# Down by a scheme of seven products, row sums on GpSimd, sample P.V in block-diagonal form

## The chip, the cores and the metric

The kernel runs on one core of one Trainium2 chip. The metric is the device time of one execution in microseconds; the median of three runs before the change is 2301.47 (2296.75 to 2304.92).

## What is computed

Two layers of a streaming encoder over 1024 prompt frames and 8 x 16 sample frames, all in float32. Each layer mixes (windowed attention beside a pooling path) and then runs a gated convolutional feed-forward. The parts that the change touches, cut from the reference:

```python
def conv_ffn(x, prev, w_up, conv_w, conv_b, w_down):
    h = x @ w_up
    ...
    gate, val = jnp.split(c, 2, axis=-1)
    y = (jax.nn.silu(gate) * val) @ w_down
    return y, full[:, -(CONV_W - 1):]
...
        keys = jnp.concatenate([cache_k, k], axis=1)
        vals = jnp.concatenate([cache_v, v], axis=1)
        attn = sink_attention(q, keys, vals, sinks, None)
...
    x = x + f
```

D_MODEL is 1024, D_FF is 2816 (22 tiles of 128). `state_conv` holds the last two up-projected rows of each of the 8 sample streams.

## The kernel before

Rows are cut into nine tiles `t` of 128: 0 to 7 are the prompt, 8 is the 128 sample rows. Every large product is made in float32 precision from operands split into a rounded part `hi` and a rest `lo`: `mm3` issues three matmuls, L152 (hi.hi), L153 (hi.lo) and L154 (lo.hi). ScalarE makes `hi` by a cast, VectorE `lo` by a subtraction.

A layer has three stages. The **mixer** runs from the input projection to the output projection; its pieces (projection columns `k`, `u`, `o`, pooling `p`, norms `n` and `m`, attention steps `L`, side loads `cw`, `sc`) have keys in `PLAN`, and `arrange` sorts them by key under their preconditions. **Up** runs over 22 tile pairs `i` of `w_up`; each takes seven products (a scheme of seven instead of eight, `PRODUCTS`) in two halves of four `mm3`, 168 matmuls 288 columns wide. VectorE adds the products up (L921), convolves (L969, two for each of gate and value), splits weights (L863) and forms weight sums (L845); `gate` multiplies and writes 128 x 1152 values to `gd` in DRAM (L979). GpSimd (`frame`, L953 to L961) copies the few border columns of the convolution. **Down** takes the 22 tiles of `w_down` in three chunks (8, 8, 6) and for each chunk all nine row tiles: `down_load` fetches a tile's rows from `gd` (L1036) and the residual from `xd` (L1041), splits the rows (L1038, L1039), and two halves of 512 columns are accumulated over the chunk's tiles, then added to the residual (L1064) and written out. `down_prep` splits the weights, one chunk ahead. The last nine units of layer 0 are sorted into the mixer of layer 1 (keys `d`).

The sample rows' attention (`sample`) has for each of 8 streams 128 cached and 16 new keys. `pt` transposes the probabilities, the cached (`pc`) and the new (`pn`) parts apart (L737), and `pv` multiplies for each stream and each of two key heads (L748, L749), with the new values brought to partitions 0 to 15 by eight small transfers (`nv`). `sconv_cols` transposes the conv state in 44 pieces of 16 rows (L1128).

All transfers are issued by SyncE, in one order. The Tile scheduler sets each engine's final order from the order of the program; tiles of one tag share a fixed number of buffers (`BUFS`): `raw` has 5, `B` 32, `W` 6, `u` 2, `ks` 1.

Of the kernel before, what the change touches and what calls it, by code (L numbers as in the profile page):

```python
# [21 lines left out]
CHUNKS = ((0, 8), (8, 16), (16, 22))  # L22
# [22 lines left out]
def arrange(tokens, limits):  # L45
# [20 lines left out]
    dict(k0=(-84.62, 2.16), u0=(-1.41, 2.89), k1=(26.68, 2.56), u1=(73.67, 4.62), o0=(92.51, 2.89), k2=(155.27, 0.46), u2=(164.87, 3.03), o1=(176.8, 5.19), o2=(235.82, 3.79), p0=(40.1, 4.11), p1=(88.06, 9.52), p2=(194.82, 13.59), n1=(-7.2, 1.2), n2=(23.98, 3.62), n3=(90.68, 0.91), m0=(218.99, 3.57), m1=(255.61, 0.33), m2=(260.5, 0.72), d=(-13.05, 1.09), L=(26.9, 49.72, 64.52, 76.71, 108.8, 144.29, 159.45, 183.94, 209.44, 246.8), cw=(232.74, 6.49), sc=(240.21, 22.72), s0=(252.76, 1.66), s1=(260.26, 12.78), v=(259.68, 0.33), w=(269.17, 1.68), upw=(310.67, 0.62), e_q=0, e_k=1, e_v=0, e_u=0, e_k2=0, e_qt=0, e_pt0=0, e_pt1=0, e_ps0=1, e_ps1=1, e_ks=0, e_w=0, e_x0=0, e_x1=1, e_x2=0),  # L66
    dict(k0=(-48.6, 0.19), u0=(35.92, 0.42), k1=(27.9, 4.13), u1=(77.36, 4.61), o0=(86.54, 2.71), k2=(147.07, 0.28), u2=(159.7, 4.59), o1=(176.8, 5.19), o2=(244.07, 2.25), p0=(43.57, 5.43), p1=(82.76, 3.73), p2=(194.08, 14.85), n1=(-25.07, 1.96), n2=(27.06, 4.21), n3=(94.98, 1.42), m0=(210.9, 1.49), m1=(221.1, 8.78), m2=(278.0, 0.99), d=(-29.34, 4.15), L=(26.9, 49.72, 64.52, 87.91, 108.8, 142.58, 160.43, 180.13, 216.19, 239.71), cw=(252.27, 13.07), sc=(271.15, 2.17), s0=(264.1, 2.05), s1=(255.17, 4.22), v=(280.24, 0.1), w=(286.24, 2.63), upw=(313.83, 2.28), e_q=0, e_k=1, e_v=1, e_u=0, e_k2=0, e_qt=0, e_pt0=0, e_pt1=0, e_ps0=1, e_ps1=1, e_ks=0, e_w=1, e_x0=1, e_x1=0, e_x2=1),
# [4 lines left out]
def encoder_kernel(ctx: ExitStack, tc: tile.TileContext, consts, x_prompt, x_sample, cache_k, cache_v,  # L72
# [15 lines left out]
    BUFS = dict(B=32, W=6, raw=5, PT=4, Q=4, u=2, sA=1, sB=1, D=2, V=5, st=15, ks=1)  # L88
# [30 lines left out]
    mhalf = cp.tile([128, 10], F32, name="mhalf")  # L119
    gain = cp.tile([128, 2, 64], F32, name="gain")  # L120
# [4 lines left out]
    xd = [dp.tile([NT, 128, DM], F32, name=f"xd{i}") for i in range(4)]  # L125
# [533 lines left out]
    def sample(l):  # L659
# [22 lines left out]
        def qk():  # L682
# [38 lines left out]
        def soft():  # L721
            s, nm, r = H["st"]
            act.activation(out=nm[:, 8:16], in_=nm[:, 0:8], func=AF.Exp, bias=snk[:, 2, 0:1])
            dve.tensor_tensor(out=r[:, 0:8], in0=s[:, 8:16], in1=nm[:, 8:16], op=ALU.add)
            dve.reciprocal(out=r[:, 8:16], in_=r[:, 0:8])
            for j in range(8):
                dve.tensor_scalar(out=H["e"][:, j], in0=H["e"][:, j], scalar1=r[:, 8 + j:9 + j], scalar2=None, op0=ALU.mult)

        def pt(i):
            def f():  # L730
                if i == 0:
                    H["pc"] = T("B", [128, 8, 128])
                    H["pn"] = T("B", [16, 8, 128])
                for nm, o, n in (("pc", 0, 128), ("pn", 128, 16)):
                    tr = P("tr")
                    for j in range(4):
                        pe.transpose(out=tr[0:n, j * 128:(j + 1) * 128], in_=H["e"][:, 4 * i + j, o:o + n], identity=ident)  # L737
                    (act.copy if n == 128 else dve.tensor_copy)(
                        out=H[nm][:, 4 * i:4 * i + 4], in_=tr[0:n].rearrange("p (s n) -> p s n", n=128))
            return f  # L740

        def pv():
            o = P("s")
            ov = o.rearrange("p (s n) -> p s n", n=64)
            for bb in range(8):
                for g in range(2):
                    r = slice(g * 64, (g + 1) * 64)
                    pe.matmul(out=ov[r, bb], lhsT=H["cv"][:, bb, r], rhs=H["pc"][:, bb, r], start=True, stop=False)  # L748
                    pe.matmul(out=ov[r, bb], lhsT=H["nv"][:, bb, r], rhs=H["pn"][:, bb, r], start=False, stop=True)  # L749
            o4 = o.rearrange("p (s h q) -> p h s q", h=4, q=16)  # L750
            state["mo", 8] = T("B", [128, 2, 4, 128], F32R)
            hi, lo = [state["mo", 8][:, i].rearrange("p h (s q) -> p h s q", q=16) for i in range(2)]
            for h in range(4):
                act.copy(out=hi[:, h], in_=o4[:, h])
            for h in range(4):
                dve.tensor_tensor(out=lo[:, h], in0=o4[:, h], in1=f32(hi[:, h]), op=ALU.subtract)
            state.pop(("qkv", 8))
            state.pop(("V", 8))

        return pr[:3], load, loadv, [kc(0), kc(1), qk, score(0), score(1), score(2), soft, pt(0), pt(1), pv]  # L760
# [210 lines left out]
    def gate(l, i):  # L971
# [50 lines left out]
    def down_prep(l, f):  # L1022
        hi, lo = [T("B", [128, DM], F32R) for _ in range(2)]
        for h in range(2):
            r = raw_tile()
            c = slice(h * 512, (h + 1) * 512)
            sync.dma_start(out=r, in_=w_down[l][f * 128:(f + 1) * 128, c])
            act.copy(out=hi[:, c], in_=r)
            dve.tensor_tensor(out=lo[:, c], in0=r, in1=f32(hi[:, c]), op=ALU.subtract)
        state["wd", f] = hi, lo  # L1030

    def down_load(l, c, t):
        a, e = CHUNKS[c]
        n = (e - a) * 128
        lo, hi = [T("B", [128, n], F32R) for _ in range(2)]
        sync.dma_start(out=f32(lo).rearrange("p (f n) -> p f n", n=128),  # L1036
                       in_=gd[l][a:e, :, t * 128:(t + 1) * 128].rearrange("f p n -> p f n"))
        act.copy(out=hi, in_=f32(lo))  # L1038
        dve.tensor_tensor(out=lo, in0=f32(lo), in1=f32(hi), op=ALU.subtract)  # L1039
        X = T("B", [128, DM])  # L1040
        sync.dma_start(out=X, in_=xd[c][t])  # L1041
        state["g", c, t] = hi, lo, X

    def down_units(l, after):
        us = []
        seq = [(c, t) for c in range(len(CHUNKS)) for t in range(NT)]
        for x, (c, t) in enumerate(seq):
            def f(x=x, c=c, t=t):
                a, e = CHUNKS[c]
                if x + 1 < len(seq):  # L1050
                    down_load(l, *seq[x + 1])
                hi, lo, X = state.pop(("g", c, t))
                for h in range(2):
                    hs = slice(h * 512, (h + 1) * 512)
                    o = P("s")
                    for ff in range(a, e):
                        w = state["wd", ff]
                        g = [v[:, (ff - a) * 128:(ff - a + 1) * 128] for v in (hi, lo)]
                        mm3(o, g, [v[:, hs] for v in w], ff == a, ff == e - 1)
                        if h == 1 and t == NT - 1:  # L1060
                            state.pop(("wd", ff))
                            if c + 1 < len(CHUNKS) and e + ff - a < CHUNKS[c + 1][1]:
                                down_prep(l, e + ff - a)
                    dve.tensor_tensor(out=X[:, hs], in0=o, in1=X[:, hs], op=ALU.add)  # L1064
# [268 lines left out]
```

## Time and profile before

| what | value |
| --- | --- |
| median of 3 runs | 2301.47 us |
| the profiled execution's own time | 2303.88 us |
| its span | 2302.1 us |
| mean granted TensorE clock | 0.989 |
| instructions | 35918 |
| Up of layer 0 | about 440 to 890 us |
| Down of layer 0 | about 890 to 1160 us, the end of it within the mixer of layer 1 |
| Down of layer 1 | about 2022 us to the end |

TensorE's matmuls are pipelined: a row's mean duration is longer than the distance from one matmul to the next, so the rate is read from the number of records in a window. Float32 matmuls that are not split (the P.V products) leave two records each.

### The profile page before, as it was taken

Reading aid. Unit: us, or ns where it says so; the run is one execution under the profiler, and the core shown is the slowest. Engines: PE = TensorE matmul, PEld = TensorE weight load, DVE = VectorE, ACT = ScalarE, POOL = GpSimd, SP = SyncE. Lnnn points to the kernel's source line nnn. Section 1 sums busy time; section 2 is a strip of 40 time slices with the busy share of each in tenths; the row PEclk is TensorE's granted clock in tenths of the full one; section 3 lists DMA queues with packets and bytes.
Section 4 is the critical chain, followed back from the end, with each engine's and each line's share of the span. In section 5 each row is a group of like instructions: output and inputs, shape, how many; then the busy total and the mean of one; then the engine's idle time right before and its main releaser. Section 6 shows DMA issues by size and latency. Waiting matters only on the chain.

```text
span 2302.1 us, 35918 instructions
## 1 busy us (share of the span) xinstructions
PE 2243.1 (97%) x13610; PEld 2003.7 (87%) x13610; DVE 1508.2 (66%) x3020; ACT 880.2 (38%) x1660; POOL 186.8 (8%) x411
## 2 busy tenths in 40 slices
PE   7999999899999999999999999989999999999999
PEld 5877867899999999888788887779999999988887
DVE  4774466988888887233446753689888888853331
ACT  3564336543434434121225543564434344421110
POOL 0100001011111110000000000011111111100000
PEclk9999999999999999999999998999999999999999
DMA  8766654222222226474765765532222222274652
GB/s 315 251 232 223 224 182 136 63 73 76 74 79 69 81 74 225 149 228 133 260 225 182 254 221 180 201 113 86 73 79 73 78 69 82 95 250 148 197 175 104
DMA packets 248206, 347.26 MB, mean 151 GB/s; under 512 B 18050, under 2 KB 176722, under 8 KB 248002
## 3 DMA queue, kind: packets, MB, share of 16 engines
q1 hardware_dynamic: 248034, 344.98, 44.8%
q8 instruction: 107, 1.75, 0.3%
q14 instruction: 65, 0.53, 0.1%
HBM read 241.44 MB, written 105.17 MB: 151 GB/s over the span
## 4 chain that ended last, share of the span: by engine, by line
PE 89%; DMA 4%; DVE 4%; ACT 2%; issue 1%; SPq 0%; POOL 0%; DVEq 0%; ACTq 0%
PE mm L152 15%; PE mm L154 15%; PE mm L153 14%; PE s L154 13%; PE s L152 13%; PE s L153 13%; PE s L642 2%; DMA raw<-in_w_in_dram 1%; DMA W<-wd0o 1%; PE tr L629 1%; PE mm L446 1%; DVE B L256 1%; PE s L590 1%; DMA W<-wd1o 1%; PE s L591 1%
## 5 line engine op out<-in xcount | busy, mean ns | idle before, releaser
L152 PE MATMUL mm<-B,W 128*128 128x288 f32 (+1 forms) x1376 | 419.6, 305 | 10.5 <-ACT B L312 7.6
L153 PE MATMUL mm<-B,W 128*128 128x288 f32 (+1 forms) x1376 | 416.4, 303 | 5.2 <-DVE B L313 5.2
L154 PE MATMUL mm<-B,W 128*128 128x288 f32 (+1 forms) x1376 | 416.6, 303 | 0.6 <-DVE W L183 0.2
L152 PE MATMUL s<-B,B 128*128 128x512 f32 x792 | 312.1, 395 | 0.9 <-DVE B L1064 0.9
L154 PE MATMUL s<-B,B 128*128 128x512 f32 x792 | 312.1, 394 | 0.0
L153 PE MATMUL s<-B,B 128*128 128x512 f32 x792 | 311.8, 394 | 0.0
L152 PEld LDWEIGHTS mm<-B,W 128*128 128x128 f32 x1376 | 259.9, 189 | 15.0 <-ACT B L312 8.9
L153 PEld LDWEIGHTS mm<-B,W 128*128 128x128 f32 x1376 | 259.9, 189 | 7.4 <-DVE B L313 5.9
L154 PEld LDWEIGHTS mm<-B,W 128*128 128x128 f32 x1376 | 259.8, 189 | 2.8 <-DVE W L183 2.2
L969 DVE SCALAR_TENSOR_TENSOR B<-B,cvp,B 128x1168 f32<-128x1168 f32 x176 | 250.4, 1427 | 1.4 <-ACT B L967 1.2
L152 PE MATMUL mm<-W,B 128*128 128x512 f32 (+1 forms) x576 | 220.4, 389 | 9.1 <-ACT B L279 2.6
L153 PE MATMUL mm<-W,B 128*128 128x512 f32 (+1 forms) x576 | 213.9, 372 | 0.0
L154 PE MATMUL mm<-W,B 128*128 128x512 f32 (+1 forms) x576 | 213.8, 375 | 0.0
L1064 DVE TENSOR_TENSOR B<-s,B 128x512 f32<-128x512 f32 x108 | 74.2, 688 | 184.9 <-PE s L154 176.4
L152 PEld LDWEIGHTS s<-B,B 128*128 128x128 f32 x792 | 148.7, 188 | 35.9 <-issue 1.3
L154 PEld LDWEIGHTS s<-B,B 128*128 128x128 f32 x792 | 148.7, 188 | 35.1 <-DVE B L1039 0.4
L862 ACT CAST W<-Q 128x512 fp32r<-128x512 f32 x132 | 82.0, 621 | 254.2 <-PE mm L154 168.5
L153 PEld LDWEIGHTS s<-B,B 128*128 128x128 f32 x792 | 148.7, 188 | 34.5
L152 PE MATMUL s<-B,W 128*128 128x288 f32 x576 | 170.9, 297 | 1.4 <-ACT B L312 1.4
L153 PE MATMUL s<-B,W 128*128 128x288 f32 x576 | 170.2, 295 | 0.0
L154 PE MATMUL s<-B,W 128*128 128x288 f32 x576 | 170.0, 295 | 0.0
L1038 ACT CAST B<-B 128x1024 fp32r<-128x1024 f32 (+1 forms) x54 | 52.8, 978 | 233.0 <-DMA B<-gd 151.8
(207 smaller groups left out, 4553.3 us busy)
## 6 DMA issues: line engine op xcount, KB each, us to landing
raw<-in_w_up_dram SPq DMA_DIRECT2D x176, 256.0 KB
xd<-B SPq DMA_DIRECT2D x63, 512.0 KB
B<-xd SPq DMA_DIRECT2D x63, 512.0 KB
gd<-B SPq DMA_DIRECT2D x44, 576.0 KB
raw<-in_w_down_dram SPq DMA_DIRECT2D x88, 256.0 KB
B<-gd SPq DMA_DIRECT2D x36, 512.0 KB
W<-wd0o SPq DMA_DIRECT2D x32, 512.0 KB
W<-wd1o SPq DMA_DIRECT2D x32, 512.0 KB
```

The source lines that it names most:

```text
L152: pe.matmul(out=out, lhsT=a[0], rhs=b[0], start=first, stop=False)
L153: pe.matmul(out=out, lhsT=a[0], rhs=b[1], start=False, stop=False)
L154: pe.matmul(out=out, lhsT=a[1], rhs=b[0], start=False, stop=last)
L256: dve.scalar_tensor_tensor(out=xn, in0=X, scalar=s[:, 2:3], in1=state["gb", which], op0=ALU.mult, op1=ALU.mult)
L446: pe.matmul(out=o, lhsT=w.raw, rhs=d, start=True, stop=True)
L590: pe.matmul(out=p[:, i, kr], lhsT=q[:, h], rhs=K[:, g, kr], start=True, stop=False)
L591: pe.matmul(out=p[:, i, kr], lhsT=q[:, h], rhs=K[:, 2 + g, kr], start=False, stop=True)
L642: pe.matmul(out=o, lhsT=V, rhs=H.pop(("p", g, kk)), start=kk == kks[0], stop=kk == 1)
L862: act.copy(out=hi, in_=src)
L969: dve.scalar_tensor_tensor(out=c, in0=h[:, j:j + 1168], scalar=cvp[:, j, ct:ct + 1], in1=c, op0=ALU.mult, op1=ALU.add)
L1038: act.copy(out=hi, in_=f32(lo))
L1064: dve.tensor_tensor(out=X[:, hs], in0=o, in1=X[:, hs], op=ALU.add)
```

## The change

Down is computed as a 2 x 2 block product: the halves of the inner dimension (tiles 0 to 10 and 11 to 21 of `gd`) and, on either side, the halves of the eight prompt tiles (rows 0 to 511, 512 to 1023) and of the 1024 output columns. Seven products (`DOWN`) replace eight. The sample tile is computed beside them in the ordinary way, in four of the products (two for either column half, with `T1` in place of `B12`). A product has 5 or 4 row tiles, its units; a unit is 11 `mm3` of 512 columns. There are 32 units a layer.

The row sums S1 to S4 are made by GpSimd as each gate tile is finished (`down_sums`): one sum for tiles 0 to 10, three for 11 to 21, written to new DRAM tiles `sd` and read back in Down; the tag `ks` gets three buffers for it. The weight sums T1 to T4 are made by VectorE during the product before (`wd_split`). Partial sums are kept in SBUF (`U`, `U7`); the residual is read and written in half rows. The last ten units of layer 0 lie in the mixer of layer 1, with six new steps `e` that split the last product's weights.

For the sample rows the new keys' probabilities are transposed at once and multiplied by a mask `own` into block-diagonal form (`pn`), so that one matmul of 512 columns serves four streams, and `nv` goes. The conv state is transposed in 11 pieces of 64 rows. `PLAN` gets new numbers throughout.

The core of the diff:

```diff
-    BUFS = dict(B=32, W=6, raw=5, PT=4, Q=4, u=2, sA=1, sB=1, D=2, V=5, st=15, ks=1)
+    BUFS = dict(B=32, W=6, raw=5, PT=4, Q=4, u=2, sA=1, sB=1, D=2, V=5, st=15, ks=3)
...
-    dict(k0=(-84.62, 2.16), u0=(-1.41, 2.89), k1=(26.68, 2.56), u1=(73.67, 4.62), ...
+    dict(k0=(-17.62, 0.24), u0=(10.61, 1.71), k1=(30.79, 2.26), u1=(78.0, 4.62), ...
...
-                for g in range(2):
-                    r = slice(g * 64, (g + 1) * 64)
-                    pe.matmul(out=ov[r, bb], lhsT=H["cv"][:, bb, r], rhs=H["pc"][:, bb, r], start=True, stop=False)
-                    pe.matmul(out=ov[r, bb], lhsT=H["nv"][:, bb, r], rhs=H["pn"][:, bb, r], start=False, stop=True)
...
+                pe.matmul(out=o, lhsT=state["V", 8], rhs=H["pn"][:, 4 * i:4 * i + 4].rearrange("p s n -> p (s n)"), start=True, stop=False)
+                for j in range(4):
+                    pe.matmul(out=o[:, j * 128:(j + 1) * 128], lhsT=H["cv"][:, 4 * i + j], rhs=H["pc"][:, 4 * i + j], start=False, stop=j == 3)
...
+    DOWN = (("B11", "A11"), ("B21", "A12"), ("T3", "S3"), ("T2", "S2"), ("T4", "A22"), ("T1", "S1"), ("B22", "S4"))
+    DSEQ = [(j, p) for j in range(7) for p in range(5 if j in (0, 1, 5, 6) else 4)]
+    PIECES = ((0, 2), (2, 4), (4, 6), (6, 8), (8, 10), (10, 11))
...
+    def down_sums(l, i, a1, a2):
...
+        def op(name, f, out, in0, in1, o):
+            pool.tensor_tensor(out=out, in0=in0, in1=in1, op=o)
+            sync.dma_start(out=sd[l][name][f], in_=out)
+        if i < HF:
+            op("S3", i, tile_(), a1, a2, ALU.subtract)
+            return
+        f = i - HF
+        s2, s1 = tile_(sd[l]["S3"][f]), tile_(gd[l][f][:, 0:512])
+        op("S2", f, s2, a2, s2, ALU.subtract)
+        op("S4", f, tile_(), a1, s2, ALU.subtract)
+        op("S1", f, s1, s1, a2, ALU.add)
...
+    def wd_split(l, j, x):
...
+            if name == "T3":
+                dve.tensor_tensor(out=w[:, k], in0=w[:, k], in1=r, op=ALU.subtract)
...
+        for h, o, v in parts:
+            act.copy(out=h, in_=v)
+            dve.tensor_tensor(out=o, in0=v, in1=f32(h), op=ALU.subtract)
...
+    def g_load(l, u):
...
+        hi, lo = [T("B", [128, 9, 128], F32R) for _ in range(2)]
+        r = T("B", [128, 2, 2, 128], F32R)
+        sync.dma_start(out=f32(lo), in_=v[:, 0:9])
+        sync.dma_start(out=f32(r[:, 1]), in_=v[:, 9:11])
...
             def f(u=u, j=j, p=p, n=n, late=late, loads=loads, splits=splits):
...
+                if u + 2 < len(DSEQ):
+                    g_load(l, u + 2)
+                if u + 1 < len(DSEQ):
+                    down_x(l, u + 1)
+                    g_split(l, u + 1)
+                down_add(l, u, None)
...
+                for x, (a, e) in enumerate(PIECES):
+                    wh, wl = state["wd", j, x]
+                    for k in range(a, e):
+                        g = (hi[:, k], lo[:, k]) if k < 9 else (r[:, 0, k - 9], r[:, 1, k - 9])
+                        mm3(o, g, (wh[:, k - a], wl[:, k - a]), k == 0, k == HF - 1)
```

What this makes of the order, at three places. GpSimd's rows in Up of layer 0, from one pair of border copies to the next, before (`V` collects the state columns to be written, `D` holds the conv state, `B` are the rows of `hb`):

```order
L953 MEMSET B_8175 128x2
L955 COPY B_8175<-D_3792 128x8x2
L953 MEMSET B_8272 128x2
L955 COPY B_8272<-D_3793 128x8x2
L960 COPY V_8054<-B_8272 128x2
L961 COPY V_8054<-B_8272 128x16
```

and after, in one of tiles 11 to 21 (`ks` are the sums):

```order
L959 MEMSET B_8455 128x2
L961 COPY B_8455<-D_3780 128x8x2
L1049 TENSOR_TENSOR ks_8374<-B_8278,ks_8374 128x512
L1049 TENSOR_TENSOR ks_8376<-ks_8376,B_8278 128x512
L959 MEMSET B_8564 128x2
L961 COPY B_8564<-D_3781 128x8x2
L1049 TENSOR_TENSOR ks_8380<-B_8278,ks_8374 128x512
L966 COPY V_8610<-B_8564 128x2
L967 COPY V_8610<-B_8564 128x16
```

Three sums now stand between the border copies, two of them ahead of the copies of the next tile. SyncE's rows at the same place, before: a gate tile's store, then the next weights.

```order
L833 DMA raw_8406<-in_w_up_dram 128x4x128
L979 DMA gd_77<-B_8008 128x1152
L833 DMA raw_8676<-in_w_up_dram 128x4x128
L833 DMA raw_8678<-in_w_up_dram 128x4x128
L833 DMA raw_8680<-in_w_up_dram 128x4x128
```

After:

```order
L839 DMA raw_8423<-in_w_up_dram 128x4x128
L985 DMA gd_84<-B_8003 128x1152
L1050 DMA sd0S_77<-ks_8100 128x512
L1050 DMA sd0S_76<-ks_8102 128x512
L1050 DMA sd0S_79<-ks_8106 128x512
L1045 DMA ks_8374<-sd0S_78 128x512
L1045 DMA ks_8376<-gd_84 128x512
L839 DMA raw_8704<-in_w_up_dram 128x4x128
L839 DMA raw_8706<-in_w_up_dram 128x4x128
```

The next weights now stand behind three stores that wait for GpSimd and two loads that wait for a free `ks` buffer. TensorE's rows where the sample P.V begins in layer 0, before (L554 and L565 are transposes for a prompt tile, `B_2841` and `B_2842` the transposed probabilities):

```order
L737 MATMUL tr_2849<-cst,B_2694 16x128
L554 MATMUL tr_2896<-cst,ks_2712 128x128 x4
L748 MATMUL s_2954<-B_2841,B_2626 64x64
L565 MATMUL tr_2903<-cst,Q_2835 128x128 x4
L749 MATMUL s_2954<-B_2842,B_2657 64x64
```

and after (L400 are transposes of the pooling state):

```order
L742 MATMUL tr_2790<-cst,PT_2744 128x128
L400 MATMUL tr_2806<-cst,B_2345 128x120
L400 MATMUL tr_2819<-cst,B_2345 128x120
L752 MATMUL s_2908<-B_2792,V_2533 128x512
L754 MATMUL s_2908<-B_2764,B_2634 128x128 x4
L752 MATMUL s_2950<-B_2792,V_2533 128x512
```

The pair L748 and L749 goes on 16 times in a layer; now two matmuls of 512 columns and eight of 128 (the last four stand further down) do the same. In Down the same listing has 2376 matmuls 512 wide on split operands before and 2112 after.

More of the change, by code (lines that the diff above doesn't have):

```diff
@@ L119, in encoder_kernel @@
     mhalf = cp.tile([128, 10], F32, name="mhalf")
+    own = cp.tile([128, 8], F32, name="own")
     gain = cp.tile([128, 2, 64], F32, name="gain")
@@ L732, in f @@
                     H["pc"] = T("B", [128, 8, 128])
[L733 to L739, printed above, removed]
@@ L740, in pt @@
-            return f
[L742 to L745, printed above, removed]
-                for g in range(2):
-                    r = slice(g * 64, (g + 1) * 64)
[L748 to L758, printed above, removed]
@@ L1018, in up_units @@
+                        if n in (2, 4):
+                            g_load(l, n // 2 - 1)
+                        if n == 4:
+                            g_split(l, 0)
                 us.append(Unit(f))
         return us
[L1022 to L1042, printed above, removed]
@@ new lines, in g_split, with down_x @@
+    def g_split(l, u):
+        hi, lo, r = state["g", u]
+        for h, o in ((hi, lo), (r[:, 0], r[:, 1])):
+            act.copy(out=h, in_=f32(o))
+            dve.tensor_tensor(out=o, in0=f32(o), in1=f32(h), op=ALU.subtract)
+    def down_x(l, u):
+        j, p = DSEQ[u]
+        if j not in (1, 4, 5, 6):
+            return
+        t = 8 if p == 4 else p if j in (4, 5) else 4 + p
+        if j == 5 and t == 8:
+            return
+        c = slice(0, 512) if j in (1, 4) else slice(512, DM)
+        if j in (5, 6) and l < DEPTH - 1:
+            X = T("B", [128, DM])
+            sync.dma_start(out=X[:, c], in_=xd[0][t][:, c])
+            sync.dma_start(out=X[:, 0:512], in_=xd[1][t][:, 0:512])
+            state["dx", u] = t, c, X[:, c], X
+        else:
+            x = T("u", [128, 512])
+            sync.dma_start(out=x, in_=xd[0][t][:, c])
+            state["dx", u] = t, c, x, None
@@ L1066, in down_units, with late_units, f @@
             us.append(Unit(f))
         return us
+    def late_units(l):
+        def f(x):
+            wd_split(l, 6, x)
+            if x + 2 < 6:
+                wd_load(l, 6, x + 2)
+        return [Unit(lambda x=x: f(x)) for x in range(6)]
     def params1(l):
         def f():
+            if "own" not in state:
+                state["own"] = True
+                dve.tensor_reduce(out=own, in_=ident.rearrange("p (b t) -> p b t", t=16), axis=mybir.AxisListType.X, op=ALU.add)
             sync.dma_start(out=gain[:, 0], in_=q_norm[l].partition_broadcast(128))
```

241 lines of the change are left out of this document (181 added, 60 removed).

## The prediction

> **What bounds the kernel now.** First the page: busy times, then the chain of work that ended last.
>
> ```profile
> span 2302.1 us, 35918 instructions
> PE 2243.1 (97%) x13610; PEld 2003.7 (87%) x13610; DVE 1508.2 (66%) x3020; ACT 880.2 (38%) x1660; POOL 186.8 (8%) x411
> ...
> PE 89%; DMA 4%; DVE 4%; ACT 2%; issue 1%; SPq 0%; POOL 0%; DVEq 0%; ACTq 0%
> ```
>
> TensorE is busy for 97% of the span and makes up 89% of the last chain. A busy TensorE need not run at its own pace, so I cut the span into stages and looked at records per us.
>
> ```profile
> core 0: us, PE busy (x) PEld busy (x) DVE busy (x) ACT busy (x) POOL busy (x), PEclk, DMA share, GB/s
> 0.00:390.00 390.00, 356.52 (x1923) 287.87 (x1923) 220.82 (x649) 185.20 (x480) 30.04 (x33) 0.98 0.66 230
> 440.00:870.00 430.00, 430.00 (x3248) 429.89 (x3247) 372.18 (x637) 169.60 (x240) 53.34 (x154) 1.00 0.24 75
> 980.00:1070.00 90.00, 90.00 (x391) 73.02 (x390) 29.95 (x39) 16.18 (x21) 0.00 (x0) 1.00 0.59 191
> 1160.00:1520.00 360.00, 355.29 (x1941) 292.29 (x1939) 215.55 (x643) 172.96 (x445) 26.66 (x23) 0.98 0.62 215
> 2120.00:2210.00 90.00, 90.00 (x390) 72.92 (x389) 27.42 (x35) 15.65 (x20) 0.00 (x0) 1.00 0.58 187
> ```
>
> The columns are time, then busy us and records by engine, the granted clock, the DMA share and GB/s. Rows 3 and 5 are Down in either layer: no idle time, full clock, 391 matmuls in 90 us, **0.230 us each**. Row 2 is Up: 0.132 us each, no idle time either, while VectorE is busy 87%. Only the mixers (rows 1 and 4) have idle time, 33.5 and 4.7 us. So in Down the number of matmuls is the time, and what is removed there is saved if the feeders keep up.
>
> **Down's products.** The groups of instructions, with busy us and mean ns behind the bar, then idle time before them:
>
> ```profile
> L152 PE MATMUL s<-B,B 128*128 128x512 f32 x792 | 312.1, 395 | 0.9 <-DVE B L1064 0.9
> L1064 DVE TENSOR_TENSOR B<-s,B 128x512 f32<-128x512 f32 x108 | 74.2, 688 | 184.9 <-PE s L154 176.4 <-DMA B<-xd 8.5
> L313 DVE TENSOR_TENSOR B<-B,B 128x1152 fp32r<-128x1152 f32 x28 | 37.2, 1351 | 6.2 <-ACT B L312 6.2
> L1029 DVE TENSOR_TENSOR B<-raw,B 128x512 fp32r<-128x512 f32 x88 | 57.3, 686 | 76.2 <-PE s L153 37.6 <-DMA xd<-B 29.9 <-ACT B L1028 8.4
> L845 DVE TENSOR_TENSOR Q<-raw,raw 128x512 f32<-128x512 f32 x88 | 60.2, 684 | 4.4 <-DMA raw<-in_w_up_dram 3.7
> L1038 ACT CAST B<-B 128x1024 fp32r<-128x1024 f32 x36 | 37.8, 1050 | 157.7 <-DMA B<-gd 96.6 <-PE s L153 61.1
> ```
>
> Before: 792 on each of three lines, 2376. After: 32 units a layer of 11 x 3, 2112. That is 264 fewer by 0.230 us = **-60.9 us**. The average matmul stays 512 wide, so its price stays.
>
> What the scheme asks of VectorE in one layer: 32 splits of 1152 (1.35 us, L313) and of 256 columns (no row; between zero and L1029's 0.69, I take 0.4), 77 weight splits (0.69), 44 weight sums (0.68, L845) and 49 row sums (0.69, L1064): 56 + 53 + 30 + 34 = 173 us, in 32 x 33 x 0.230 = 243 us. Today it is 30 in 90. Worst are the products of four units (30.4 us) during which T4 or T1 is made: 4 x 1.75 + 22 x 0.69 + 8 x 0.69 = 27.7 us. That still fits. Today L1064 waits for TensorE (176 us), not the other way. ScalarE's casts, 32 of L1038's kind and 77 half as wide, come to some 90 us of the 243 and are hidden by the same matmuls.
>
> What it asks of the DMA: rows 3 and 5 move 191 GB/s at a share of 0.59, so a full share is 324 GB/s. After, layer 1 moves 32 x 0.72 MB of rows, 88 x 0.26 MB of weights and 36 x 0.26 MB of residual: 56 MB in 243 us, 229 GB/s, a share of 0.71. Landing times are the weak point; the third row below is from the waits of SyncE's queue in that stage (us in total, times, longest):
>
> ```profile
> 2125.66 0.81 SPq L1036 DMA_DIRECT2D B<-gd  x1
> ...
> 2134.66 1.05 ACT L1038 CAST B<-B 128x1024 fp32r<-128x1024 f32 x1 [5.74 <-DMA B<-gd]
> ...
> SPq L1027 <- DVE B L1029: 59.0, 23, 10.7
> ```
>
> Row 1 is a load as SyncE issues it, row 2 the cast that waits for it: 9.0 us for 0.5 MB. The new load is 0.72 MB and issued two units (15.2 us) ahead of its matmuls. It fits with a few us to spare, unless the queue is held: row loads stand behind weight loads, and these wait until VectorE frees a raw buffer, 23 times and up to 10.7 us already today. I put **+3 us** on this, between 0 (no row shows Down faster than 0.230) and +20 (0.3 us in each of 64 units).
>
> **Row sums on GpSimd, in Up.** 88 tensor_tensor of 128x512: one for each of tiles 0 to 10, three for each of tiles 11 to 21. A tile of Up has 168 matmuls, 22.2 us; of that VectorE is idle 13%, **3.0 us**. No GpSimd row has this shape; the nearest, and VectorE's additions from PSUM:
>
> ```profile
> L961 POOL COPY V<-B 128x16 f32<-128x16 f32 x88 | 76.2, 866 | 1.3 <-DVE B L921 0.4
> L505 POOL TENSOR_TENSOR st<-st,mhalf 128x10 f32<-128x10 f32 x18 | 36.2, 2013 | 403.8 <-DVE st L504 323.7 <-DVE st L716 57.9 <-DVE D L425 22.3
> L955 POOL COPY B<-D 128x16 f32<-128x16 f32 x88 | 22.5, 256 | 21.6 <-ACT D L1129 21.6
> L921 DVE TENSOR_TENSOR PT<-mm,PT 128x288 f32<-128x288 f32 x176 | 79.2, 452 | 12.9 <-PE mm L154 12.0
> ```
>
> And the timeline shows that the two engines get in each other's way:
>
> ```profile
> 603.20 1.34 POOL L961 COPY V<-B 128x16 f32<-128x16 f32 x1
> ...
> 603.05 1.42 DVE L969 SCALAR_TENSOR_TENSOR B<-B,cvp,B 128x1168 f32<-128x1168 f32 x1
> 604.39 0.68 DVE L863 TENSOR_TENSOR sB<-Q,sA 128x512 fp32r<-128x512 f32 x1
> ```
>
> A copy of 16 columns takes 1.34 us here and ends at 604.54, when the L969 that began before it has ended (604.47). GpSimd seems to wait for a VectorE instruction with two SBUF inputs; whether VectorE waits for a long GpSimd one, these short copies cannot show. A sum of length P, with full exclusion, takes 3P from VectorE in a late tile and costs TensorE 3P - 3.0 us, times 22 late tiles (early ones, with one sum, have room up to P = 3.0). P = 0.26 (L955): nothing. P = 0.68, VectorE's own price of this shape (L845): nothing. P = 2.01 (L505): 66 us. L845 has the shape, L505 the engine and the two inputs; I take the middle, 1.35 us. Full exclusion then gives 1.05 x 22 = 23 us. But a third of VectorE's time in a tile goes to additions from PSUM (L921: twelve of 288 columns and four of about half, 0.45 each for the wide ones, some 6.3 of 19.2 us), and where a third of the sums falls on those, 2.7 us fit into 3.0. I take **+6 us**.
>
> The Trainium skill, "SBUF — State Buffer", Who interferes with whom, speaks against this edit: a VectorE instruction with two SBUF inputs and a GpSimd one that reads SBUF shut each other out for the whole instruction. "GPSIMD Engine Reference", section 3.1, gives 4497 ns for 2048 columns; an estimate from that is 1.12 us for 512, and the formula would then give 0.4 x 22 = 8 us, a sum 2 us higher. The copy above agrees with the rule for GpSimd's side; VectorE's side no row here shows.
>
> SyncE now waits for GpSimd before it stores a sum, and the next Up weights stand behind that store. In the waits of SyncE's queue between 500 and 870 us:
>
> ```profile
> SPq L833 <- DVE W L863: 124.5, 30, 6.6
> ```
>
> L833, the same weight load, already waits for a free raw buffer 30 times, 4.2 us on average. A store that comes a sum or two later hides in that wait, so I add nothing; without it, P per late tile would come on top.
>
> **Sample P.V and conv state, in the mixers.** TensorE's timeline in the mixer of layer 0:
>
> ```profile
> 277.78 1.03 PE L737 MATMUL tr<-cst,B 128*128 128x128 f32 x8
> ...
> 281.07 0.33 PE L748 MATMUL s<-B,B 128*64 128x64 f32 x2
> ...
> 284.40 0.32 PE L749 MATMUL s<-B,B 16*64 16x64 f32 x2
> 284.65 1.82 PE L737 MATMUL tr<-cst,B 128*128 128x128 f32 x8
> ...
> 361.77 1.02 PE L642 MATMUL s<-PT,V 128*128 128x512 f32 x2
> 362.63 1.03 PE L292 MATMUL tr<-cst,B 128*128 128x128 f32 x8
> 363.46 0.50 PE L152 MATMUL mm<-W,B 128*128 128x512 f32 x1
> L1128 PE MATMUL tr<-cst,B 16*128 16x16 f32 x88 | 5.6, 210 | 0.0
> ```
>
> From 281.07 to 284.65 stand 28 small matmuls, 0.128 us each; 128 in both layers are 16.4 us. In their place come 8 records 512 wide (L642: 0.43 each, 3.4 us) and 32 records 128 wide (L292: 0.10 each, 3.3 us). 14 transposes fewer (L737, 0.13) are 1.8 us; 88 conv-state transposes (0.064) against 22 (0.10) are 3.4 us. In all 14.9 us less of TensorE's work, where it also waits for others: all of it or none may come through. I take half, **-7 us**. The new keys move the rest of the mixers; I put 0 on them, between -15 and +15: idle time there is 33.5 + 4.7 = 38 us, of which a new order can win a part, and lose as much.
>
> **Sum.** 2303.9 (the profiled execution's own time; its span is 2302.1) - 60.9 - 7 + 6 + 3 = 2245.0. That execution lies 2.4 us above the median of the runs shown, 2301.5: **2242 us** for the median.
>
> **Rivals.**
> 1. *GpSimd's sums make VectorE the bound of late Up.* P = 1.7 with full exclusion: 2.1 x 22 = 46 instead of 6, **2282**. For it: the wait at 603.20, VectorE at 87%. Against: a third of VectorE's work reads PSUM.
> 2. *Down is starved.* Landing times past 15 us stop VectorE, which works in order and also empties PSUM: +20 instead of 3, **2259**. For it: a share of 0.71 and the 9.0 us landing. Against: two units of lookahead.
> 3. *The mixers gain fully and nothing stalls:* -14.9 for -7, -10 by the keys, no 6 and no 3: **2215**. For it: VectorE's free 3.0 us and Down's 0.230 without a gap. Against: it needs four good ends at once.
> 4. *Slower:* the sums run at GpSimd's slow pace, P = 3 us or more. Each late tile then needs 9 us of shared access against 3 free: 6 x 22 = 132 in place of 6, **2368**. It decides from P = 2.0: 3.0 x 22 = 66, less the 6 taken, is the 59 us that the sum gains. For it: L505, 2.0 us for ten columns. Against: that is a power, and L955 copies in 0.26.
>
> That the products are not saved is excluded: the program's order has 2112.
>
> **Chances.** Forecast 0.50 (2228 to 2256), rival 3 0.17, rival 2 0.15, rival 1 0.13, rival 4 0.05. The range reaches to rivals 3 and 1, **2214 to 2282**, and leaves out rival 4 and the tails of the keys. Faster by over 0.3% (about what a measurement here can tell) 0.94, same 0.01, slower 0.05.
>
> **What the changed profile would show.** Down windows with some 391 records in 90 us and no idle TensorE: the first term holds; fewer, and the idle time's releaser names rival 2. In late Up the window of 22 us with less than 168 records, and VectorE's two-input rows longer than 1.42 and 0.68: rival 1. A P other than 0.7 to 1.4 us makes that term wrong. Mixer windows more than 15 us off these make the keys' term wrong.

## The result and the profile after

The changed kernel takes **2242.5 us** (2241.5 to 2246.3, four runs) against 2301.9 (2296.8 to 2304.9) for the kernel before, timed in turn: a ratio of 0.9747, 95% interval 0.9726 to 0.9768. The profiled execution has a span of 2240.7 us, 61.4 less than the one before.

The page of the changed kernel; the last line is the group of one of the three matmuls of Down:

```profile
span 2240.7 us, 36002 instructions
...
PE 85%; DMA 6%; DVE 5%; ACT 2%; issue 1%; SPq 0%; POOL 0%; DVEq 0%; ACTq 0%
...
L154 PE MATMUL s<-B,B 128*128 128x512 f32 x704 | 279.6, 397 | 4.1 <-ACT B L1133 2.7
```

704 for 792 on each of three lines: the 264 matmuls are gone. The mean of one is as before, but the idle time ahead of them has grown from 0.9 to 4.1 us, and the casts of Down's rows (L1133) end 2.7 of it. The windows by stage, with the columns known from before:

```profile
0.00:366.00 366.00, 333.57 (x1744) 270.31 (x1745) 221.99 (x658) 163.89 (x431) 28.19 (x29) 0.97 0.68 236
...
640.00:880.00 240.00, 240.00 (x1806) 239.90 (x1805) 224.02 (x347) 95.51 (x137) 77.63 (x117) 1.00 0.41 135
886.00:975.00 89.00, 85.55 (x360) 68.46 (x361) 69.73 (x93) 38.52 (x56) 7.08 (x6) 0.98 0.90 279
980.00:1070.00 90.00, 90.00 (x390) 72.99 (x389) 60.88 (x87) 34.70 (x49) 0.00 (x0) 1.00 0.76 239
...
2080.00:2170.00 90.00, 90.00 (x389) 72.82 (x388) 62.24 (x87) 36.96 (x54) 0.00 (x0) 1.00 0.65 200
```

Row 2 is late Up: no idle TensorE, though VectorE has gone to 93%. Rows 4 and 5 are Down well under way, at 390 and 389 records in 90 us, the pace of before. Row 3 is Down's first 89 us: 360 records where the pace allows 386, 3.5 us of idle time, a granted clock under 1 and the DMA engines at a share of 0.90. In the same layout, by the start times of the matmuls in the two traces:

| stretch (us) | before | after | difference |
| --- | --- | --- | --- |
| start to the end of the first Up tile, layer 0 | 423.6 | 415.1 | -8.5 |
| the next 20 Up tiles, layer 0 | 446.6 | 448.2 | +1.6 |
| the last Up tile, layer 0 | 22.3 | 23.5 | +1.2 |
| Down of layer 0 and mixer of layer 1, to the end of its first Up tile | 659.4 | 629.4 | -30.0 |
| the next 20 Up tiles, layer 1 | 446.8 | 447.8 | +1.0 |
| the last Up tile, layer 1 | 22.4 | 24.3 | +1.9 |
| Down of layer 1 | 275.7 | 248.2 | -27.5 |
| tail | 5.3 | 4.3 | -1.0 |

Each layer's Down has 132 matmuls fewer at 0.230 us, 30.4 us. Two things hide in the table, then: the mixers give more than it seems, and each **crossing from Up to Down** costs time that it did not cost before. I measure a crossing's loss as the last Up tile's time over the mean of tiles 11 to 20, plus what the matmul steps of Down's first three blocks have over the median step. Before, that is 0.4 and 0.5 us in the two layers; after, **6.4 and 5.3**. (A median step that is off by a nanosecond moves such a loss by half a microsecond.)

So the 61.4 us come about as -60.8 (products), some -13 (both mixers: -8.5, and -30.0 + 30.4 - 4.9 = -4.5), some +11 (the crossings), +2.6 (20 Up tiles in each layer) and -1.0 (the tail). Of the 2.6, 1.6 stand in layer 0, where each tile takes some 0.08 us more, and most of the 1.0 in layer 1 is its second tile alone, 23.1 us for 22.2, in which TensorE once waits 0.57 us for VectorE's additions.

### The profile page after: what moved, and what is told of

It reads as the page before. It is cut to its first block, busy times and chain, and to the rows that moved or that the text cites. A ratio compares the mean times of both kernels' runs of the same rounds, so it can differ in the third digit from the quotient of the medians.

```text
span 2240.7 us, 36002 instructions
## 1 busy us (share of the span) xinstructions
PE 2169.5 (97%) x13178; PEld 1945.5 (87%) x13178; DVE 1712.6 (76%) x3234; ACT 943.5 (42%) x1749; POOL 326.6 (15%) x499
## 4 chain that ended last, share of the span: by engine, by line
PE 85%; DMA 6%; DVE 5%; ACT 2%; issue 1%; SPq 0%; POOL 0%; DVEq 0%; ACTq 0%
PE mm L154 15%; PE mm L155 15%; PE mm L156 15%; PE s L156 11%; PE s L154 11%; PE s L155 11%; PE s L644 2%; DMA raw<-in_w_down_dram 1%; DMA raw<-in_w_in_dram 1%; PE tr L631 1%; PE mm L448 1%; DMA W<-wd1o 1%; PE s L592 1%; DMA xd<-u 1%; PE tr L294 1%
## 5 line engine op out<-in xcount | busy, mean ns | idle before, releaser
L154 PE MATMUL s<-B,B 128*128 128x512 f32 x704 | 279.6, 397 | 4.1 <-ACT B L1133 2.7
L156 PE MATMUL s<-B,B 128*128 128x512 f32 x704 | 279.2, 397 | 2.8 <-DVE B L1134 2.8
L155 PE MATMUL s<-B,B 128*128 128x512 f32 x704 | 278.6, 396 | 0.0
L1133 ACT CAST B<-B 128x256 fp32r<-128x256 f32 (+1 forms) x128 | 97.3, 780 | 204.7 <-DMA B<-gd 70.5
L154 PEld LDWEIGHTS s<-B,B 128*128 128x128 f32 x704 | 133.2, 189 | 36.2 <-ACT B L1133 5.3
L156 PEld LDWEIGHTS s<-B,B 128*128 128x128 f32 x704 | 133.0, 189 | 34.9 <-DVE B L1134 3.6
L155 PEld LDWEIGHTS s<-B,B 128*128 128x128 f32 x704 | 133.1, 189 | 30.7
L869 DVE TENSOR_TENSOR W<-Q,W 128x512 fp32r<-128x512 f32 x132 | 134.6, 1020 | 20.6 <-ACT W L868 20.6
```

The lines of the kernel that those rows point to most:

```text
L154: pe.matmul(out=out, lhsT=a[0], rhs=b[0], start=first, stop=False)
L155: pe.matmul(out=out, lhsT=a[0], rhs=b[1], start=False, stop=False)
L156: pe.matmul(out=out, lhsT=a[1], rhs=b[0], start=False, stop=last)
L869: dve.tensor_tensor(out=lo, in0=src, in1=f32(hi), op=ALU.subtract)
L1133: act.copy(out=h, in_=f32(o))
```

## The experiments

Each is the changed kernel with one edit, unless said otherwise. Times are medians; ratios are to the kernel before on the same chip.

### Where the mixers' gain comes from

`old_pv` puts the former P.V back, `old_keys` the former `PLAN`, and `pv_alone` adds the new P.V and the packed conv state to the kernel before:

```diff
-                pe.matmul(out=o, lhsT=state["V", 8], rhs=H["pn"][:, 4 * i:4 * i + 4].rearrange("p s n -> p (s n)"), start=True, stop=False)
+                    pe.matmul(out=ov[r, bb], lhsT=H["cv"][:, bb, r], rhs=H["pc"][:, bb, r], start=True, stop=False)
+                    pe.matmul(out=ov[r, bb], lhsT=H["nv"][:, bb, r], rhs=H["pn"][:, bb, r], start=False, stop=True)
```

```diff
-    dict(k0=(-17.62, 0.24), u0=(10.61, 1.71), k1=(30.79, 2.26), u1=(78.0, 4.62), ...
+    dict(k0=(-84.62, 2.16), u0=(-1.41, 2.89), k1=(26.68, 2.56), u1=(73.67, 4.62), ...
```

> The changed kernel with the sample P.V as it was before (32 matmuls into 64-row halves, four 16-row transposes for the new tokens, eight scalings); the keys, the packed conv state and Down are those of the change. Theory one, that the sample P.V in block-diagonal form is what shortens the mixers (10.5 us by the two traces, the interleaved first Up tiles counted in): the mixer windows go back by 6 to 10 us and the time is 2248 to 2253. Theory two, that the keys or the packed conv state do it: 2240 to 2246, with the mixer windows where the change has them. The keys were set for the new list of steps, so an order that doesn't suit the old list may add up to 5 us of its own; a time above 2253 would say so.

> The changed kernel with the keys that order the mixers' steps as they were before; P.V, conv state and Down are those of the change. Theory one (P.V makes the mixer gain, keys only follow): 2240 to 2246, the same time within 0.15%. Theory two (the keys make it): 2248 to 2256, with the loss in the mixer windows (0 to 366 and some 1165 to 1516 less the Down part) and none in Up or Down.

> The kernel before with the new sample P.V and the packed conv-state columns alone; old keys, old Down with eight products, no sums. Theory one (P.V and conv state make the mixer gain whatever the keys): 8 to 11 us under the kernel before, ratio 0.9952 to 0.9965. Theory two (the keys make it): within 3 us of the kernel before, ratio 0.9987 to 1.0013. Half and half, as the prediction took it (-7): ratio 0.9965 to 0.9975.

| kernel | us | ratio to before (95%) |
| --- | --- | --- |
| old_pv | 2249.84 | 0.9776 (0.9763 to 0.979) |
| old_keys | 2241.91 | 0.9743 (0.9728 to 0.9757) |
| pv_alone | 2296.28 | 0.9974 (0.9964 to 0.9984) |

By the whole time, P.V is worth 7 us both ways and the keys nothing. In `pv_alone` neither theory held: 6.6 us lies between them, where the prediction's half had it. The mixer of layer 0 shows more. Its windows from the start to the first Up product, in the kernel before and in `pv_alone` (that of the change stands above):

```profile
0.00:376.00 376.00, 343.96 (x1818) 276.58 (x1819) 207.47 (x633) 178.31 (x467) 28.79 (x30) 0.98 0.67 233
```

```profile
0.00:373.00 373.00, 336.45 (x1764) 271.61 (x1765) 207.84 (x626) 179.62 (x467) 28.32 (x29) 0.98 0.67 234
```

The new P.V takes 7.5 us of TensorE's work out of this mixer, half of the 14.9 that the prediction counted for two layers. With the old keys 4.5 us of that come back as waiting: TensorE idles 36.5 us in place of 32.0, and the mixer ends 3 us earlier. With the new keys (333.57 of 366) it idles 32.4 and ends 10 us earlier. With the new keys and the former P.V (`old_pv`) it ends 10.8 us later than in the change. In `old_keys` it ends 5 us later than in the change, and still the whole time is the same, since its Up tiles in layer 0 run faster, of which more below: 444.8 us for the 20 tiles and not 448.2. So "P.V alone does it" holds for the work; the keys let the work's end come through, and their share is known to a few us only.

### What the sums on GpSimd cost

One kernel leaves the sums out (its Down reads rows of `gd` in their place), one makes them on VectorE, two make two and three times as many on GpSimd:

```diff
-        down_sums(l, i, g[:, 512:1024], g[:, 0:512])
```

```diff
-            pool.tensor_tensor(out=out, in0=in0, in1=in1, op=o)
+            dve.tensor_tensor(out=out, in0=in0, in1=in1, op=o)
```

```diff
+        def extra(out, n):
+            for _ in range(n):
+                pool.tensor_tensor(out=out, in0=a1, in1=a2, op=ALU.subtract)
...
+            extra(s3, 1)
...
+        extra(s4, 3)
```

> The changed kernel without the sums and their stores: Down's S products read rows of the gated activations in place of the sums. What the sums cost in all is the difference. Theory one (slack hides them): 2238 to 2243, late tiles at 22.3, VectorE back at 86 to 87%, its 512-wide subtractions beside them at 0.68 to 0.69 us. Theory two (the prediction's +6 stands, but another term was off by as much): 2234 to 2238. The last Up tile's stall stays (23.4 and 24.3 us) if it is made by Down's first loads, and goes if the sums make it.

> The changed kernel with the S sums made on VectorE and not on GpSimd. A VectorE subtraction of this size took 0.68 us (the 512-wide rows of before), so a late Up tile gets 2.0 us of it, where the trace of the change shows 1.45 us of lengthening for the three GpSimd sums (VectorE 86.6% to 93% of a 22.34-us tile, slack 1.55 us). Theory one (VectorE's slack is what hides the sums, wherever they run): VectorE 95 to 96% of late Up, late tiles at 22.3 to 22.5, time 2240 to 2250. Theory two (GpSimd is off VectorE's path and VectorE is near its bound, so sums on VectorE stand ahead of the Up work in its order): late tiles 22.6 to 23.2, 2252 to 2265.

> The changed kernel with twice as many GpSimd sums per tile (2 in an early tile, 6 in a late one; the additional results are overwritten). Theory one (each sum lengthens VectorE's work by about 0.48 us, and 1.55 us of slack is left in a late tile): VectorE 98 to 100% of late Up, late tiles at 22.4 to 22.8, time 2243 to 2256. Theory two (each sum takes VectorE for its whole 1.3 to 1.7 us, as the prediction had it with 1.35): three more take 4.0 us where 1.55 is left, 2.5 us in each of 22 late tiles, 2298. Theory three (no exclusion, VectorE only slowed by chance): 2242.

> Three times the GpSimd sums (3 in an early tile, 9 in a late one). Theory one (0.48 us of VectorE for each): VectorE is past its slack by 1.35 us in each of 22 late tiles, late tiles 23.4 to 24.2, time 2265 to 2285. Theory two (the whole span of each): 8.1 us more against 1.55, 6.5 us in each late tile, 2385. Theory three (no exclusion): 2242.

| kernel | us | ratio to before (95%) |
| --- | --- | --- |
| no_sums | 2243.29 | 0.9742 (0.9718 to 0.9766) |
| sums_dve | 2240.16 | 0.9726 (0.9702 to 0.975) |
| the change itself | 2242.51 | 0.9747 (0.9726 to 0.9768) |
| sums_x2 | 2246.20 | 0.9753 (0.9724 to 0.9781) |
| sums_x3 | 2317.23 | 1.0064 (1.0044 to 1.0084) |

The sums cost nothing that can be measured, on either engine; twice as many cost at most a few us, three times as many 75. VectorE's busy time (the sixth number) in 200 us of late Up tells why: in turn no_sums, sums_dve, the change, sums_x2, sums_x3.

```profile
660.00:860.00 200.00, 200.00 (x1506) 199.90 (x1505) 171.73 (x292) 78.01 (x111) 24.86 (x72) 1.00 0.23 75
```

```profile
660.00:860.00 200.00, 200.00 (x1506) 199.90 (x1505) 182.83 (x318) 78.52 (x111) 29.09 (x71) 1.00 0.40 134
```

```profile
660.00:860.00 200.00, 200.00 (x1506) 199.90 (x1505) 188.23 (x291) 77.34 (x111) 65.87 (x99) 1.00 0.40 133
```

```profile
660.00:860.00 200.00, 199.66 (x1501) 199.32 (x1501) 195.79 (x289) 75.06 (x110) 104.38 (x120) 1.00 0.39 127
```

```profile
660.00:860.00 200.00, 181.77 (x1323) 178.75 (x1322) 193.49 (x261) 66.65 (x99) 127.72 (x127) 0.98 0.35 112
```

Without sums VectorE is at 86%; with 27 sums on GpSimd in this stretch it is at 94%, 16.5 us more: **each sum on GpSimd takes 0.61 us of VectorE's free time**. Made by VectorE itself, the same sums take 11.1 us of it, 0.41 us each. That is less than the 0.68 us that such a sum's row shows there, since VectorE's rows overlap when they stand close: they add up to 188.6 us in no_sums for 171.7 of busy time, and to 205.8 for 182.8 in sums_dve, where fewer pauses are left. In sums_x2 VectorE stands at 98%, and TensorE first loses a few tenths. The further sums take 7.6 us, only 0.3 us each, so 0.61 is no fixed price: at 0.61 six sums would need 3.7 us in a late tile that has 3.2 free, and cost some 11 us in all (4 were measured). In sums_x3 TensorE loses 18 us of 200. The toll sits in a few rows. GpSimd's sums and two of VectorE's groups in this stretch of the change, behind them the first of these two in no_sums:

```profile
L1049 POOL TENSOR_TENSOR ks<-B,ks 128x512 f32<-128x512 f32 x18 | 23.2, 1287 | 33.0 <-DVE B L982 33.0
L1049 POOL TENSOR_TENSOR ks<-ks,B 128x512 f32<-128x512 f32 x9 | 15.7, 1745 | 0.0
...
L869 DVE TENSOR_TENSOR W<-Q,W 128x512 fp32r<-128x512 f32 x27 | 33.0, 1222 | 5.2 <-ACT W L868 5.2
L851 DVE TENSOR_TENSOR Q<-Q,raw 128x512 f32<-128x512 f32 x8 | 11.3, 1414 | 0.0
```

```profile
L869 DVE TENSOR_TENSOR W<-Q,W 128x512 fp32r<-128x512 f32 x27 | 18.6, 688 | 7.2 <-ACT W L868 7.2
```

A VectorE subtraction with two SBUF inputs that meets a sum waits for it: the mean of 1222 ns mixes 18 rows of 1.41 to 1.57 us with nine of 0.69. The three sums of one late tile, and the VectorE rows beside them:

```profile
694.79 1.29 POOL L1049 TENSOR_TENSOR ks<-B,ks 128x512 f32<-128x512 f32 x1 [3.77 <-DVE B L982]
696.04 1.74 POOL L1049 TENSOR_TENSOR ks<-ks,B 128x512 f32<-128x512 f32 x1
...
698.35 1.29 POOL L1049 TENSOR_TENSOR ks<-B,ks 128x512 f32<-128x512 f32 x1
...
694.84 0.45 DVE L927 TENSOR_TENSOR PT<-mm,PT 128x288 f32<-128x288 f32 x1
695.21 1.43 DVE L869 TENSOR_TENSOR W<-Q,W 128x512 fp32r<-128x512 f32 x1
696.56 0.45 DVE L927 TENSOR_TENSOR PT<-mm,PT 128x288 f32<-128x288 f32 x1
696.92 1.41 DVE L851 TENSOR_TENSOR Q<-Q,raw 128x512 f32<-128x512 f32 x1
698.26 0.44 DVE L927 TENSOR_TENSOR PT<-mm,PT 128x288 f32<-128x288 f32 x1
698.63 1.56 DVE L869 TENSOR_TENSOR W<-Q,W 128x512 fp32r<-128x512 f32 x1
```

The additions from PSUM (L927) keep their 0.45 us beside a sum; each subtraction after them is held. This is the side of the rule of the Trainium skill ("SBUF — State Buffer", Who interferes with whom) that the trace before could not show: GpSimd shuts VectorE out too. The Trainium skill's "Perfetto Trace Analysis", Optimizing Scalar/DVE Operations, warns that moving work between these two engines may not help as they share a read port. The trace agrees: the same sums took 0.61 us of VectorE's free time on GpSimd and 0.41 on VectorE, and the kernel's time was the same.

I expected 2265 to 2285 of sums_x3 and missed by 32 us: most of its late tiles take 25 to 27 us, not 23.4 to 24.2. Besides VectorE's share another wait came up, between 720 and 860 us; below it the shares of that stretch in the chain that ended last:

```profile
ACT B L973 <- POOL ks L1049: 34.1, 6, 6.5
...
by line: POOL ks L1053 25.9%; issue 15.9%; POOL ks L1049 13.3%; DVE W L869 9.7%; ACT B L973 5.8%; DMA raw<-in_w_up_dram 5.6%; DVE PT L927 5.3%; ACT W L868 4.5%; DVE B L975 2.9%; DVE Q L851 2.8%; POOL V L966 1.6%; DVE B L927 1.2%; ACT PT L93
```

ScalarE's first step of the convolution (L973) waits for GpSimd in six of six tiles, and each time the end of the tile's last sum releases it. It is no border copy that it waits for: in the program L973 writes into the `B` buffer that this sum still reads. With nine sums that buffer comes free late, and GpSimd's sums (L1049, and L1053, which makes the additional ones) are 39% of the chain. How the loss divides between this wait and VectorE's share was not separated by an experiment.

### What makes the crossing slow

TensorE at the first crossing in the change, then the casts of Down's first raw weights there (a group's idle time and what ended it):

```profile
885.50 0.30 PE L156 MATMUL mm<-B,sB 128*128 128x288 f32 x1
886.72 0.50 PE L154 MATMUL s<-B,B 128*128 128x512 f32 x1 [0.92 <-ACT B L1133]
887.06 0.39 PE L155 MATMUL s<-B,B 128*128 128x512 f32 x1
888.83 0.79 PE L156 MATMUL s<-B,B 128*128 128x512 f32 x1 [1.38 <-DVE B L1134]
889.42 0.63 PE L154 MATMUL s<-B,B 128*128 128x512 f32 x1
889.85 0.63 PE L155 MATMUL s<-B,B 128*128 128x512 f32 x1
```

```profile
L1106 ACT CAST B<-raw 128x512 fp32r<-128x512 f32 x11 | 6.5, 621 | 11.2 <-DMA raw<-in_w_down_dram 11.2
```

TensorE waits for the split of the first rows, which stands on ScalarE and VectorE behind casts that wait 11.2 us for raw weights. SyncE meanwhile has issued the six `W` loads (L1068, 2.9 MB) between 857 and 885 us, though T3 is the first to use them, and VectorE makes it between 920 and 936 us. The sums are not the cause: without them (`no_sums`) the last Up tiles still take 23.5 and 23.9 us, and the loss is 5.0 and 5.3 us. One kernel moves the last splits of the first block behind the last Up products, one puts the `W` loads behind the last raw load of the first block, one does both; the change itself ran beside them.

```diff
-                        for x in range(6):
+                        for x in range(4):
                             if x // 2 == n - 1:
                                 wd_split(l, 0, x)
...
+                        if n == 6:
+                            wd_split(l, 0, 4)
+                            wd_split(l, 0, 5)
```

```diff
+        if j == 0 and x == 5:
+            state["lastb11"] = state["lastraw"]
...
-        sync.dma_start(out=w, in_=wd_block(l, "B22", x))
+        with tc.issue_after(state["lastb11"].ins):
+            sync.dma_start(out=w, in_=wd_block(l, "B22", x))
```

> The changed kernel unaltered, timed on the chip of the three that follow, for comparison: 2241 to 2246.

> The changed kernel with the splits of the last two pieces of Down's first block moved from the fourth step of the last Up tile to its end, behind the last products. Theory one (VectorE, in order, waits in those splits for late raw weights, and the additions that free PSUM stand behind): the last Up tiles take 22.4 to 22.8 and not 23.4 and 24.3, the first Down unit may lose 1 us each; 2238 to 2242. Theory two (the stall is the loads' lateness, wherever it is waited for): the same 1.1 to 2.1 us stand in the first Down unit, 2241 to 2246.

> The changed kernel with the six 0.5-MB loads of the third block (wanted some 38 us later) put behind the last raw load of Down's first block on SyncE. Theory one (those loads make the raw weights late, so that the ScalarE casts idle 0.7 to 4.4 us in the last Up tile): the idle time before the casts falls under 1 us in all, the last Up tile takes 22.4 and the gaps of 1.5 us and the half-clock stretch at Down's start go: 4 to 8 us less in the two layers, 2234 to 2239. Theory two (five raw buffers and their release set the raw loads' pace, the large loads don't matter): 2241 to 2246.

> Both edits together. If late raw loads are the cause, it is no better than the loads alone (2234 to 2239); if VectorE's order is, no better than the splits alone; if each takes a part, 1 to 3 us under the better of the two.

| kernel | us | ratio to before (95%) | loss at the crossings, layers 0 and 1 |
| --- | --- | --- | --- |
| after_again | 2241.85 | 0.9738 (0.972 to 0.9756) | 6.5, 4.8 |
| split_late | 2241.29 | 0.9728 (0.9715 to 0.9742) | 6.2, 4.9 |
| w_late | 2246.49 | 0.975 (0.9733 to 0.9768) | 8.8, 6.5 |
| both | 2239.35 | 0.9722 (0.9709 to 0.9735) | 6.7, 8.2 |

Each of the three clears the last Up tile (22.2 to 22.4 us), and each pays about the same or more in all, now in Down's first blocks: the loads' lateness is waited for elsewhere, the second theory of `split_late`. In w_late that was against my first theory: the `W` loads now stood among and ahead of the raw loads of the *second* block, and the gaps came at 898, 907 and 961 us. (The 2.5 us of `both` are not a smaller loss; its mixers and its Up tiles in layer 1 were a little faster.) So two readings were left: the bytes are too many, wherever they stand, or they stand too close together. The last kernel puts the same loads behind the fifth piece of the second block's raw loads, two units into Down:

```diff
+        if j == 1 and x == 4:
+            state["b21"] = ins
...
-        sync.dma_start(out=w, in_=wd_block(l, "B22", x))
+        with tc.issue_after(state["b21"].ins):
+            sync.dma_start(out=w, in_=wd_block(l, "B22", x))
...
-                if j == 0:
-                    for x in range(p, 6 if p == 4 else p + 1):
+                if j == 0 and p > 2:
+                    for x in range(3 * p - 9, 3 * p - 6):
```

> The changed kernel with the same six loads put behind the fifth piece of the second block's raw loads, two units into Down, some 25 us before their first use; the splits stay where the change has them. The loss at the crossing (last Up tile, and matmul steps over the median pace in the first three blocks) was 6.4 and 5.3 us in the two layers of the change, 6.3 and 4.9 with the splits moved, 8.8 and 6.5 with the loads right behind the first block. Theory one (a burst: these 2.75 MB pull transfers together at a share of 0.9 and over, and the raw weights of the first two blocks come late by it): the loss falls to 1 to 3 us in each layer, 2232 to 2238. Theory two (bytes: some 35 MB go in the 140 us around the crossing where 23.5 went before, so each order only moves the stall): the loss stays at 5 to 8 us in each layer, with the gaps at another place, such as the second and third block, 2240 to 2247.

**2231.77 us** (2230.86 to 2235.32), a ratio of 0.969 (0.9677 to 0.9703): 10.1 us under the change as it was timed beside the last three kernels (11 us by the two ratios), and the loss at the crossings is 1.2 and 0.8 us. The same windows around the crossing, from the change and then from w_later:

```profile
850.00:886.00 36.00, 35.79 (x270) 35.53 (x268) 28.34 (x47) 13.84 (x22) 12.54 (x18) 1.00 0.67 223
886.00:905.00 19.00, 16.90 (x66) 13.14 (x67) 16.11 (x19) 10.73 (x17) 7.08 (x6) 0.91 1.06 339
905.00:930.00 25.00, 25.00 (x109) 20.29 (x108) 19.44 (x29) 13.71 (x21) 0.00 (x0) 1.00 0.97 292
930.00:955.00 25.00, 25.00 (x109) 20.23 (x108) 21.53 (x31) 8.43 (x11) 0.00 (x0) 1.00 0.89 276
955.00:980.00 25.00, 23.64 (x102) 18.64 (x101) 17.57 (x22) 9.51 (x13) 0.00 (x0) 1.00 0.68 206
```

```profile
850.00:886.00 36.00, 36.00 (x273) 35.98 (x273) 31.26 (x52) 14.90 (x23) 13.07 (x18) 1.00 0.56 191
886.00:905.00 19.00, 18.45 (x81) 14.49 (x80) 18.12 (x19) 12.03 (x18) 6.90 (x5) 1.00 0.84 257
905.00:930.00 25.00, 25.00 (x109) 20.29 (x108) 14.20 (x21) 9.53 (x16) 0.00 (x0) 1.00 1.06 339
930.00:955.00 25.00, 25.00 (x109) 20.18 (x108) 23.12 (x33) 10.71 (x13) 0.00 (x0) 1.00 0.98 311
955.00:980.00 25.00, 25.00 (x110) 20.23 (x109) 19.55 (x27) 11.43 (x16) 0.00 (x0) 1.00 0.85 269
```

The peak of 339 GB/s is still there, but 20 us later, when the first block's weights have long been split, and TensorE has no idle time beside it. The bytes between 850 and 990 us, for the change and for w_later, have not become fewer (the kernel before moved 23.47 MB there):

```profile
DMA packets 35363, 34.76 MB, mean 248 GB/s; under 512 B 1924, under 2 KB 24600, under 8 KB 35352
```

```profile
DMA packets 36861, 35.51 MB, mean 254 GB/s; under 512 B 1956, under 2 KB 26098, under 8 KB 36850
```

So it is neither the bytes nor the burst by itself, but its place: loads that nobody used for some 50 to 60 us were issued among and ahead of loads that the next instructions waited for. Whether these came late by SyncE's order or because the transfers shared the DMA engines was not separated.

## Why the prediction came out at the time

2242 was predicted and 2242.5 measured, but that close a hit is luck: three of its terms were off and made up for each other (-13 for -7, 0 for +6, +11 for +3), and the 2.5 us by which the sum of 2245.0 still missed the profiled execution were covered by the 2.4 us taken off for the median, where the changed kernel's profiled execution lies anyway.

- **Products, -60.9.** Right: 264 fewer, the Down windows at 390 and 389 records in 90 us, -60.8.
- **Sample P.V and conv state, -7, and the keys, 0.** Mis-sized: together some -13, where "all of it or none may come through" gave -14.9 to 0 for the first. P.V and conv state took 7.5 us of TensorE's work from the mixer of layer 0, and with the new keys no waiting came in its place. Rival 3 had -14.9 and -10 for the two, about twice what came.
- **Row sums, +6.** The step that failed is the last one, "I take +6". The duration was near (1.35 us taken; 1.29 and 1.75 measured, three in a late tile 4.3 us, a mean of 1.44, just above the 0.7 to 1.4 that the prediction allowed), and the mutual waiting was right. But what a sum takes of VectorE's free time is 0.61 us, as not all of its time falls on an instruction with two SBUF inputs (the rows at 694.79 us): 1.8 us in a late tile that has 3.0 free. The working had 2.7 us against 3.0, that is nothing, and then put 6 us beside it. VectorE at 94% and TensorE without a gap is the answer, and sums_x2, with 98%, shows how near the edge it is. The weight loads behind the sums' stores, put at nothing, cost nothing: no_sums takes the same time.
- **Down's landing times, +3.** The term for late loads was +11, and it lay at another place: not in the steady units, whose share of 0.65 to 0.76 was forecast at 0.71 and leaves no gap, but at the crossing, where the working looked at the loads' rate in the middle of Down and not at what SyncE would issue at its start. That rows stand behind weight loads was named; that the six early `W` loads would be the ones in front was not seen in the order.
- **Rivals.** 1 and 4 needed a toll of P for each sum; it was 0.61. Of rival 1's two signs one came (VectorE rows of 1.4 to 1.6 us for 0.69), but TensorE had no idle time in late Up. With three times the sums the kernel does run slower than the one before, 2317 us, by this mechanism and ScalarE's wait together. Rival 2 (late loads, 17 us more) came about at 11 us, at the crossing and not in the steady units.
- The +2.6 of the Up tiles was in no term. The sums don't make it in layer 0: no_sums takes the same 448.2 us for its 20 tiles.

## What to carry to other kernels

When a change puts a prefetch into a queue, look at what the queue issues at the *start* of the stage that uses it, and hold back every load whose first use is far off behind those that the next units wait for: here that was 10 us for the same bytes, and holding them back behind the first block alone gained nothing. Work moved to GpSimd is not free for VectorE: price it at what it takes from VectorE's two-input instructions, count the free time in the tile, and find where it stops fitting by running two and three times the work. Ask also which buffers it holds. A total that comes out right proves none of its terms.

## What the runs showed of the hardware

- A sum of 128x512 on GpSimd took 1.29 to 1.75 us and added 0.61 us to VectorE's busy time; made by VectorE, the same sum added 0.41 us (its row shows 0.68). The next three sums of a tile added only 0.3 us each.
- After two waits of 0.92 and 1.38 us between 885.8 and 888.8 us, the matmuls of 512 columns followed each other at 0.43 us in place of 0.23 for some 3 us, at a granted clock of 0.50 from 889 to 892 us. That is some 1.6 us of the first crossing's 6.4. A single longer wait did not always do that: in split_late one of 1.78 us, ending at 895.27, was followed by steps of 0.23 us. What decides was not tried.
- VectorE's 128x512 subtractions have rows of 0.68 us and follow each other at 0.60 us, so a sum of row durations overstates its work.
- The same Up code has another pace in another program. With the old keys the stretch from 640 to 880 us holds 1821 matmuls and not 1806, at the same clock of 1.00 and without idle time:

```profile
640.00:880.00 240.00, 240.00 (x1821) 239.92 (x1820) 224.76 (x350) 96.67 (x138) 78.98 (x117) 1.00 0.41 135
```

That is 22.23 us for a late tile against 22.41. The change itself, profiled twice, gave 22.41 in layer 0 and 22.35 in layer 1 both times, so it belongs to the program. Nor do the sums make it: in layer 0 no_sums takes 448.2 us for 20 tiles as the change does, and pv_alone, which has none either, 444.8. Over these 20 tiles it is worth 3.4 us, as much as an edit in the mixer, and its cause stays open.
